# A two-layer trunk on one core: the mask by ScalarE, joint head products, rows' inverse roots by ScalarE, and turns between two blocks of the output projection

## The chip, the cores and the metric

The kernel runs on one core of one Trainium2 chip. The metric is the time of one execution on the device in microseconds (us). Engines are named as in the profile: PE is TensorE's matmul, PEld its weight loads, DVE VectorE, ACT ScalarE, SP the queue that issues nearly all DMAs.

## The reference

Two layers (DEPTH = 2) work on x, 256 rows by 2048 columns, all in float32. Cut to what matters here:

```
shift, scale, gate = split(c @ w_ada + b_ada)
h = rms_norm(x, g_pre) * (1 + scale) + shift
u, g_pool, q, k, v, g_diff = split(h @ w_in)             # 2048 -> 6144 columns
pool = multiscale_pool(u, w_pool, pool_scale) * silu(g_pool)     # 4 groups
q, k = rope(q), rope(k)                                  # 8 heads, 2 maps of 64 columns each
s = q k^T / 8, set to -1e30 where chunk(key) > chunk(query), chunks of 64 rows
p = softmax(s);  a = p[map 0] - lam * p[map 1]
diff = rms_norm(a v, subln_g) * (1 - lam_init) * silu(g_diff)
y = concat(pool, diff) @ w_out                           # 2048 -> 2048 columns
x = x + (1 + gate) * rms_norm(y, g_post)
rms_norm(x, g) = x * rsqrt(mean(x * x) + 1e-6) * g
```

## The kernel before

Rows are held as two tiles of 128 (st = 0, 1). The big products, h @ w_in and y = cat @ w_out, run in a split float32: each weight tile (`raw`, 128x1024) is cast to a rounded high part on ACT (`whi`), the rest is taken on DVE (`wlo`), and PE adds three products, high by high, high by low and low by high, of 128x512 each. A *unit* is two such 128-row slices of a 512-column block `nb`: 12 products of 512 columns for both row tiles. `plan()` writes the order of all units by hand: 12 blocks of w_in in each layer, then w_out. Lines 489 to 499 lay out w_out: the first half of the sum (k of the four pool groups, cat 0 to 3) for blocks 0, 1, 2, 3, then the second half (the four pairs of heads, cat 4 to 7) for blocks 2, 3, 0, 1. In the last eight units of a layer (a group of their own) row tile 0 runs through all before row tile 1.

All other work is written as tasks (`Flow`, lines 132 to 333). A planner at build time holds a clock for each engine, estimates when each task's next instruction can start from what it reads and writes (`depends`, line 273), and picks the one to be issued next by a due time. The order so found is the fixed order in which each engine takes its instructions on the chip; an instruction that isn't ready there holds up those behind it on its engine. The unit stream (`products`) has the latest due of all, so that on PE whatever else is ready goes first. `depends` makes the first product into a PSUM bank wait until that bank is free, bank by bank.

Each head of the attention (`head`, line 1202) takes two of four PSUM banks (`self.banks`), one for each map m. Query tile t = 0 sees 128 keys, t = 1 sees 256. Lines 1211 to 1213 make four float32 products with 64 rows of the array each, in the order (m, t) = (0,0), (1,0), (0,1), (1,1); each shows as two MATMUL rows, `psb<-zz,zz`. Lines 1214 to 1216 then add the mask by one bf16 product for each map, `psb<-neg,ind`. DVE takes the negated row maximum of each part (`top`), ACT the exponential with its sum (`exp`). `heads` (line 1233) runs two heads as a pair, at most two pairs at a time. It subtracts the maps, transposes them, multiplies by v, takes the rows' inverse roots (`rsqrt` with n = 4, on DVE), gates, transposes again and writes cat 4 to 7.

`rms` (line 796) makes the inverse root of each row's mean square for the norms before and after a layer: a `tensor_reduce` and then `rsqrt` with n = 1, in all eight short instructions on DVE (a start value from the bits, three Newton steps of two instructions). It is called six times: for x at the start (two row tiles), for y and for the next x between the layers (two each), and for y at the end (two). `residual` (line 1389) calls it after y; the last one is followed by x = y * r + x and by the stores.

Of the kernel before, what the change touches and what calls it, by code (L numbers as in the profile page):

```python
# [13 lines left out]
BF16 = mybir.dt.bfloat16  # L14
# [6 lines left out]
DEPTH = 2  # L21
S = 256
D = 2048
P = 128
# [58 lines left out]
class Task:  # L83
# [3 lines left out]
    def __init__(self, flow, f, due):  # L87
        self.flow, self.f, self.due = flow, f, due
        self.ask, self.cond, self.error, self.over = None, None, None, False
# [40 lines left out]
class Flow:  # L130
# [8 lines left out]
    TABLES = ((AF.Exp, 1), (AF.Silu, 2), (AF.Sin, 3))  # L139
# [29 lines left out]
    def due(self, due):  # L169
        self.cur.due = due if callable(due) else lambda: due  # L170

# [75 lines left out]
    def turn(self, key, op, outs, ins, total, table):  # L247
# [7 lines left out]
        a.names = {r[0] for r in a.outs + a.ins}  # L255
# [19 lines left out]
    def depends(self, a):  # L275
        t = 0.0
        for r in a.ins:
            t = max(t, self.latest(self.wrote, r))
            if a.key != "tensor" and r[0].startswith(("acc", "ps")):
                t = max(t, self.latest(self.used, r))  # L280
        for r in a.outs:
            if a.key != "tensor" or not self.wrote.get(r[0]):
                t = max(t, self.latest(self.used, r))
        return t
# [113 lines left out]
class Kern:  # L398
# [39 lines left out]
    def plan(self):  # L438
# [25 lines left out]
        for l in range(DEPTH):  # L464
# [35 lines left out]
            while l + 1 < DEPTH and kp_at[l + 1][self.START[l + 1] - 1] is None:  # L500
                take()
        for l, n in enumerate(self.TURN):
# [62 lines left out]
    def run(self):  # L565
# [9 lines left out]
        self.pairs, self.turning, self.mixed = 0, 0, [0] * DEPTH  # L575
# [6 lines left out]
    def begin(self):  # L582
# [17 lines left out]
        self.sqj = self.const([P, NB], "sqj", BF16)  # L600
        self.arrived, self.squared = [False] * NST, False
# [68 lines left out]
    def mask(self):  # L670

        v = self.nc.vector
# [100 lines left out]
    def rsqrt(self, ss, n, mul=None, end=None):  # L773


        v = self.nc.vector
        x, h = ss, self.small([P, n], "rh")
# [3 lines left out]
        if mul:  # L781
            x = self.small([P, n], "rx")
            v.tensor_scalar(x, ss, 0.5 * mul, 0.5 * EPS, op0=ALU.mult, op1=ALU.add)
        v.tensor_scalar(yi, x.bitcast(I32), -0.5, 0x5F3759DF - (1 << 22) - (1 << 31), op0=ALU.mult, op1=ALU.add)
        for i in range(3):
            if n == 1:
                v.scalar_tensor_tensor(h, y, x, y, op0=ALU.mult, op1=ALU.mult)
            else:
                v.tensor_tensor(h, y, y, op=ALU.mult)
                v.tensor_tensor(h, h, x, op=ALU.mult)  # L790
            if i == 2 and end is not None:
                v.tensor_tensor(y, y, end, op=ALU.mult)
# [409 lines left out]
    def head(self, l, h0, qT, kT, st, p):  # L1202

        nc, v = self.nc, self.nc.vector
# [24 lines left out]
    def heads(self, l, hp):  # L1229
# [232 lines left out]
```

## Time and profile before

| | us |
|---|---|
| runs of the kernel before | 826.73, 826.27, 825.59; median 826.27 |
| the profiled execution, its own time | 826.03 |
| its span, from first to last instruction | 824.2 |
| PE, DVE, ACT busy in it | 803.8, 703.2, 535.7 |

A row of a timeline gives the start in us from the span's start, the time taken, the engine, the instruction with what it writes and reads, how many of them were merged, and in brackets the idle time before it with what ended that. All lines of the kernel are recorded at line 125, a helper's, so tiles tell instructions apart: `accc` holds sums of the big products, `psb` the banks of the small ones, `zz` the blocks of h @ w_in, `catz` the input of w_out, `sm`, `rs`, `rh`, `ry` short columns. Matmuls are pipelined, so that what a matmul costs is read from start to start and not from its own duration.

### The profile page before, as it was taken

To read this page: it belongs to the slowest core of one execution; us is meant where nothing else is said; L and a number is where in the kernel's file an instruction comes from. 1 tells how busy PE (TensorE), PEld (TensorE's weight loads), DVE (VectorE), ACT (ScalarE), POOL (GpSimd) and SP (SyncE) were. 2 spreads that over 40 slices of the span, in tenths; PEclk is the share of its full clock that TensorE was granted. 3 is DMA by queue.
4 is the path that set the end of the run, shared out by engine and by line. 5 is a ranking of instruction groups with operands and counts; after the bars stand their busy time and mean duration, and the time that the engine had idled before them with its cause. 6 is when DMAs were issued, how large, how long until landed. Compare 5 with 4: busy or idle time off the path is not lost.

```text
span 824.2 us, 11857 instructions
## 1 busy us (share of the span) xinstructions
PE 803.8 (98%) x4064; PEld 662.2 (80%) x4064; DVE 703.2 (85%) x1262; ACT 535.7 (65%) x930; POOL 0.2 (0%) x4
## 2 busy tenths in 40 slices
PE   7999999999999999999999999999999999999995
PEld 3688788888998777788878889888898887778884
DVE  7999999899989889899899899879888997678814
ACT  3779998777665566766388557657565466677511
POOL 0000000000000000000000000000000000000000
PEclk9999999999999999999999999999999999999998
DMA  9999997999998776877898599999999974545303
GB/s 346 407 410 409 408 373 278 395 392 371 390 375 298 258 236 223 275 257 254 299 337 316 201 391 366 335 368 366 335 393 381 349 257 118 183 139 179 125 1 102
DMA packets 68383, 245.07 MB, mean 297 GB/s; under 512 B 7746, under 2 KB 8034, under 8 KB 68066
## 3 DMA queue, kind: packets, MB, share of 16 engines
q1 hardware_dynamic: 68034, 244.14, 81.5%
q8 instruction: 32, 0.52, 0.2%
q10 hardware_dynamic: 288, 0.17, 0.1%
q14 instruction: 29, 0.23, 0.1%
HBM read 242.17 MB, written 2.11 MB: 296 GB/s over the span
## 4 chain that ended last, share of the span: by engine, by line
PE 94%; DVE 3%; ACT 1%; DMA 1%; issue 0%; SPq 0%; DVEq 0%; ACTq 0%
PE accc L125 85%; PE psb L125 9%; DVE adaz L125 1%; DMA adaz<-in_w_ada 1%; DVE wloz L125 0%; ACT halfz L125 0%; ACT zz L125 0%; DVE x L125 0%; DVE rh L125 0%; DVE ry L125 0%; PE accb L125 0%; ACT accc L125 0%; DVE zz L125 0%; DVE halfz L125 0%; ACT hz L125 0%
## 5 line engine op out<-in xcount | busy, mean ns | idle before, releaser
L125 PE MATMUL accc<-whiz,hz 128*128 128x512 f32 x1256 | 397.8, 394 | 2.5 <-ACT accc L125 1.2
L125 DVE TENSOR_TENSOR wloz<-rawz,whiz 128x1024 fp32r<-128x1024 f32 x253 | 304.1, 1220 | 16.1 <-ACT whiz L125 13.1
L125 ACT CAST whiz<-rawz 128x1024 fp32r<-128x1024 f32 x253 | 260.5, 1055 | 85.7 <-DMA rawz<-in_w_in 55.6
L125 PEld LDWEIGHTS accc<-whiz,hz 128*128 128x128 f32 x1256 | 234.4, 188 | 56.3 <-DVE hz L125 3.4
L125 DVE SCALAR_TENSOR_TENSOR adaz<-adaz,cb 128x1024 f32<-128x1024 f32 x192 | 231.0, 1220 | 25.7 <-DMA adaz<-in_w_ada 23.5
L125 PE MATMUL accc<-wloz,hz 128*128 128x512 f32 x628 | 246.6, 393 | 0.0
L125 PE MATMUL accc<-whiz,catz 128*128 128x512 f32 x512 | 165.6, 398 | 0.9 <-DVE catz L125 0.9
L125 PEld LDWEIGHTS accc<-wloz,hz 128*128 128x128 f32 x628 | 118.0, 188 | 24.7 <-DVE wloz L125 1.0
L125 PEld LDWEIGHTS accc<-whiz,catz 128*128 128x128 f32 x512 | 94.9, 188 | 21.4 <-DVE catz L125 1.3
L125 PE MATMUL accc<-wloz,catz 128*128 128x512 f32 x256 | 101.7, 397 | 0.0
L125 ACT COPY zz<-accc 128x512 f32<-128x512 f32 x121 | 70.1, 588 | 35.7 <-PE accc L125 35.3
L125 ACT COPY accc<-zz 128x512 f32<-128x512 f32 x106 | 62.7, 592 | 24.8 <-DVE halfz L125 19.4
L125 PE MATMUL accc<-hz,whiz 128*128 128x256 f32 x512 | 72.2, 283 | 0.0
L125 PEld LDWEIGHTS accc<-hz,whiz 128*128 128x128 f32 x512 | 66.7, 192 | 0.7
L125 PEld LDWEIGHTS accc<-wloz,catz 128*128 128x128 f32 x256 | 48.2, 188 | 10.0 <-issue 0.5
L125 PE MATMUL accc<-hz,wloz 128*128 128x256 f32 x256 | 41.4, 283 | 0.0
L125 ACT ACTIVATE sqj<-accc 128x512 bf16<-128x512 f32 x16 | 9.6, 600 | 41.8 <-PE accc L125 41.6
L125 PEld LDWEIGHTS accc<-hz,wloz 128*128 128x128 f32 x256 | 35.4, 192 | 0.0
L125 DVE TENSOR_TENSOR yz<-accc,Gz 128x512 f32<-128x512 f32 x16 | 10.8, 688 | 28.6 <-ACT sqj L125 28.5
L125 ACT ACTIVATE halfz<-psb,sm 128x128 f32<-128x128 f32 (+1 forms) x64 | 26.5, 421 | 10.9 <-DVE sm L125 7.2
L125 PE MATMUL psb<-consts,halfz 128*128 128x128 f32 x176 | 30.4, 276 | 3.0 <-ACT halfz L125 3.0
L125 PEld LDWEIGHTS psb<-consts,halfz 128*128 128x128 f32 x176 | 22.2, 141 | 11.5 <-ACT halfz L125 5.4
(109 smaller groups left out, 530.0 us busy)
## 6 DMA issues: line engine op xcount, KB each, us to landing
adaz<-in_w_ada SPq DMA_DIRECT2D x192, 512.0 KB, 6.8
rawz<-in_w_in SPq DMA_DIRECT2D x189, 512.0 KB, 6.5
rawz<-in_w_out SPq DMA_DIRECT2D x64, 512.0 KB, 4.2
x<-in_x SPq DMA_DIRECT2D x2, 1024.0 KB, 8.5
wpz<-in_w_pool SPq DMA_DIRECT2D x4, 512.0 KB, 7.2
Gz<-gate SPq DMA_DIRECT2D x4, 512.0 KB, 4.8
out<-x SPq DMA_DIRECT2D x8, 256.0 KB, 2.8
rawz<-in_w_in SPq DMA_DIRECT2D x6, 256.0 KB, 8.9
```

What stands on the lines that cost most here:

```text
L125: return f(*args, **kw)
```

## The change

1. **Mask.** `mask` makes one float32 tile `neg` of 64x2x64. In `head` the two mask products are gone; after a map's last product ACT copies `neg` over the masked quarter of both parts of its bank, and `top` reads the bank after that.
2. **Joint head products.** A new `until` tells the planner to hold the next instruction of a task until given tiles are written and given banks are free. `head` names q, k and both its banks ahead of its first product. It adds no instruction and no wait on the chip.
3. **Inverse roots.** `rms` is now: a negated `tensor_reduce` on DVE, a square root on ACT, a reciprocal and one Newton step of two instructions on DVE. ACT's table for the root is loaded by a dummy root (`root_table`): at the start, and in each layer after the eighth head's exponentials, due 6 us ahead of the layer's last eight units of w_out, once the gate blocks have been through Silu. The planner's list of tables has a new entry for it. `rsqrt` for the heads keeps its instructions.
4. **Turns.** The first eight units of w_out in each layer are sorted by k // 4: blocks 0 and 1 with cat 0 and 1, then blocks 0 and 1 with cat 2 and 3.

```diff
+    TABLES = ((AF.Exp, 1), (AF.Silu, 2), (AF.Sin, 3), (AF.Sqrt, 4))
...
+    def until(self, *tiles, free=()):
+        self.cur.also = [(self.wrote, self.region(x)) for x in tiles] + [(self.used, self.region(x)) for x in free]
...
     def depends(self, a):
...
+        for d, r in a.also:
+            t = max(t, self.latest(d, r))
         return t
...
     def plan(self):
...
+            i = next(i for i, u in enumerate(units) if (u.w, u.l) == ("w_out", l))
+            units[i : i + 8] = sorted(units[i : i + 8], key=lambda u: u.k // 4)
...
     def begin(self):
...
+        self.one, self.junk1 = self.const([P, 1], "one"), self.const([P, 1], "junk1")
+        nc.vector.memset(self.one, 1.0)
+        self.root_table()
...
     def mask(self):
-        self.ind = self.const([P, P], "ind", BF16)
-        v.memset(self.ind, 0.0)
-        self.neg = self.const([P, 2, CHUNK], "neg", BF16)
-        v.memset(self.neg, NEG)
-        for m in range(2):
-            v.memset(self.ind[m * DQK : m * DQK + 1, 0:CHUNK], 1.0)
+        self.neg = self.const([CHUNK, 2, CHUNK], "neg")
+        self.nc.vector.memset(self.neg, NEG)
...
-    def rms(self, parts):
-        s1 = self.small([P, 1], "rs1")
-        self.nc.vector.tensor_reduce(s1, parts, axis=AX.X, op=ALU.add)
-        return self.rsqrt(s1, 1)
+    def rms(self, parts, due=None):
+        v, f = self.nc.vector, self.f
+        s1, y, h = (self.small([P, 1], n) for n in ("rs", "ry", "rh"))
+        v.tensor_reduce(s1, parts, axis=AX.X, op=ALU.add, negate=True)
...
+        self.nc.scalar.activation(y, s1, AF.Sqrt, scale=-2.0)
+        v.reciprocal(y, y)
...
+        v.scalar_tensor_tensor(h, y, s1, y, op0=ALU.mult, op1=ALU.mult)
+        v.scalar_tensor_tensor(y, h, 1.5, y, op0=ALU.add, op1=ALU.mult)
+        return y
+
+    def root_table(self):
+        self.nc.scalar.activation(self.junk1, self.one, AF.Sqrt)
...
     def head(self, l, h0, qT, kT, st, p):
...
+        f.until(qT, kT, free=bank)
         for t, o in ((0, slice(0, P)), (1, slice(P, 3 * P))):
             for m, r in maps:
-                nc.tensor.matmul(bank[m][:, o], qT[r, t, c], kT[r, 0 : t + 1, c], start=t == 0, stop=False, skip_group_check=True)
-        for m, r in maps:
-            o = bank[m].rearrange("p (t k) -> p t k", t=2)[:, :, CHUNK:P]
-            nc.tensor.matmul(o, self.ind[r, :], self.neg[r, :, :], start=False, stop=True, skip_group_check=True)
+                nc.tensor.matmul(bank[m][:, o], qT[r, t, c], kT[r, 0 : t + 1, c], start=t == 0, stop=t == 1, skip_group_check=True)
+        for m in range(2):
+            nc.scalar.copy(bank[m].rearrange("p (t k) -> p t k", t=2)[0:CHUNK, :, CHUNK:P], self.neg)
...
     def heads(self, l, hp):
...
+                self.weighed[l] += 1
+                if self.weighed[l] == H:
+                    f.due(self.need(next(u for u in self.units if u.group == 2 * l + 2), 6.0))
+                    f.wait(lambda: all((l, b) in self.done for b in GP + GD))
+                    self.root_table()
```

## Rows read from the trace of the kernel before

**Rows 1.** The page's busy times, and of its slices over the span the clock granted to TensorE (tenths of full speed).

```profile
PE 803.8 (98%) x4064; PEld 662.2 (80%) x4064; DVE 703.2 (85%) x1262; ACT 535.7 (65%) x930; POOL 0.2 (0%) x4
...
PEclk9999999999999999999999999999999999999998
```

**Rows 2.** The page's chain of work that ended last, as shares of the span by engine.

```profile
PE 94%; DVE 3%; ACT 1%; DMA 1%; issue 0%; SPq 0%; DVEq 0%; ACTq 0%
```

**Rows 3.** Busy time by stretch of 40 us, in both of which heads run. The columns: the stretch, its length, then busy us and in brackets the number of instructions of PE, PEld, DVE, ACT and POOL, the clock granted to TensorE, the share of DMA and GB/s.

```profile
340.00:380.00 40.00, 40.00 (x216) 31.84 (x215) 34.75 (x109) 27.18 (x71) 0.00 (x0) 1.00 0.86 286
...
720.00:760.00 40.00, 40.00 (x230) 31.84 (x229) 31.14 (x90) 30.00 (x89) 0.00 (x0) 1.00 0.51 154
```

**Rows 4.** Timeline of PE in the plain stream of w_out, late in layer 1.

```profile
801.02 0.39 PE L125 MATMUL accc<-wloz,catz 128*128 128x512 f32 x1
...
801.70 0.39 PE L125 MATMUL accc<-wloz,catz 128*128 128x512 f32 x1
```

**Rows 5.** Timeline of PE where a head's first product stands by itself: the first such place of the trace, then one head of layer 0 with both its places, then the last of the 13 such places.

```profile
274.12 0.48 PE L125 MATMUL psb<-zz,zz 64*128 64x128 f32 x2
...
321.70 0.40 PE L125 MATMUL accc<-wloz,catz 128*128 128x512 f32 x1
322.02 0.48 PE L125 MATMUL psb<-zz,zz 64*128 64x128 f32 x2
322.44 0.73 PE L125 MATMUL accc<-whiz,catz 128*128 128x512 f32 x2
...
323.70 0.40 PE L125 MATMUL accc<-wloz,catz 128*128 128x512 f32 x1
324.03 0.70 PE L125 MATMUL psb<-zz,zz 64*128 64x128 f32 x5
...
324.93 0.73 PE L125 MATMUL accc<-whiz,catz 128*128 128x512 f32 x2
...
745.31 0.49 PE L125 MATMUL psb<-zz,zz 64*128 64x128 f32 x2
```

**Rows 6.** Timeline of PE around a head of layer 1 whose products stand together.

```profile
694.60 0.40 PE L125 MATMUL accc<-wloz,hz 128*128 128x512 f32 x1
694.93 0.93 PE L125 MATMUL psb<-zz,zz 64*128 64x128 f32 x8
695.69 0.22 PE L125 MATMUL psb<-neg,ind 64*128 64x128 bf16 x2
695.84 0.73 PE L125 MATMUL accc<-whiz,hz 128*128 128x512 f32 x2
```

**Rows 7.** Timeline of DVE at a head's first maximum in layer 1.

```profile
748.73 0.62 DVE L125 TENSOR_REDUCE sm<-psb 128x1 f32<-128x128 f32 x2 [1.14 <-PE psb L125]
```

**Rows 8.** Groups of instructions with shapes kept apart: busy us, mean ns of one, idle us before them. ACT's table loads, and the short instructions nearest to the new ones.

```profile
L125 ACT ACT_TABLE_LOAD x6 | 7.7, 1283 | 5.4 <-DVE sm L125 2.7 <-DMA cb<-in_c 2.6
...
L125 ACT COPY grow<-psb 16x128 f32<-16x128 f32 x2 | 0.5, 248 | 0.2 <-PE psb L125 0.2
...
L125 ACT ACTIVATE lamexp<-lamdots 128x4 f32<-128x4 f32 x1 | 0.2, 193 | 0.0
```

**Rows 9.** Timeline of PE and DVE where layer 0 of w_out waits for cat.

```profile
319.26 0.68 DVE L125 TENSOR_TENSOR catz<-zz,catz 128x512 fp32r<-128x512 f32 x1
...
319.99 0.73 PE L125 MATMUL accc<-whiz,catz 128*128 128x512 f32 x2 [0.88 <-DVE catz L125]
```

**Rows 10.** Timeline of DVE and PE between the layers: three weight tiles' rest on DVE, and PE's wait for the low part of h.

```profile
418.47 3.48 DVE L125 TENSOR_TENSOR wloz<-rawz,whiz 128x1024 fp32r<-128x1024 f32 x3
...
422.21 0.73 PE L125 MATMUL accc<-whiz,hz 128*128 128x512 f32 x2 [0.93 <-DVE hz L125]
```

**Rows 11.** Timeline of DVE at the end: the first two of the inverse root's eight instructions, which stand in a row, and the final x behind them.

```profile
815.98 0.15 DVE L125 TENSOR_REDUCE rs<-yss 128x1 f32<-128x5 f32 x1
816.16 0.15 DVE L125 TENSOR_SCALAR ry<-rs 128x1 int32<-128x1 int32 x1
...
817.70 2.74 DVE L125 SCALAR_TENSOR_TENSOR x<-yz,ry,x 128x512 f32<-128x512 f32 x4
```

**Rows 12.** The start: issues of w_ada's tiles in the first 30 us (count, KB each, median us from issue to landing), the issues of the fifth to the eighth tile (merged), DVE on the eighth, and PE's wait behind it.

```profile
adaz<-in_w_ada SPq DMA_DIRECT2D x12, 512.0 KB, 9.5
9.28 4.15 SPq L125 DMA_DIRECT2D adaz<-in_w_ada  x4
22.92 1.22 DVE L125 SCALAR_TENSOR_TENSOR adaz<-adaz,cb 128x1024 f32<-128x1024 f32 x1
25.28 3.70 PE L125 MATMUL accc<-rawz,halfz 128*128 128x512 f32 x8 [1.23 <-ACT halfz L125]
```

**Rows 13.** Timeline of ACT at a table load: the load and the instruction behind it.

```profile
31.74 1.28 ACT L125 ACT_TABLE_LOAD   x1
33.03 0.35 ACT L125 ACTIVATE cos<-halfz,halfpi 128x64 f32<-128x64 f32 x1
```

**Rows 14.** Timeline of DVE in layer 1: the last pair of heads' inverse roots, first and last instruction (those between are left out), and the last part of cat; of PE the last product of the kernel.

```profile
762.55 0.16 DVE L125 TENSOR_SCALAR rx<-sm 128x4 f32<-128x4 f32 x1
...
770.42 0.16 DVE L125 SCALAR_TENSOR_TENSOR ry<-rh,ry 128x4 f32<-128x4 f32 x1
...
775.85 0.75 DVE L125 SCALAR_TENSOR_TENSOR catz<-psb,cols,catz 128x512 fp32r<-128x512 f32 x1 [0.69 <-ACT catz L125]
...
814.17 0.39 PE L125 MATMUL accc<-whiz,catz 128*128 128x512 f32 x1
```

More of the change, by code (lines that the diff above doesn't have):

```diff
@@ L88, in __init__ @@
         self.flow, self.f, self.due = flow, f, due
-        self.ask, self.cond, self.error, self.over = None, None, None, False
+        self.ask, self.cond, self.error, self.over, self.also = None, None, None, False, []
         self.go = threading.Semaphore(0)
@@ L138 @@
     COST = {"vector": (0.09, 1.08e-3, 0.02, 0.15), "scalar": (0.11, 0.92e-3, 0.13, 0.18), "gpsimd": (0.25, 2.3e-3, 0.0, 0.15)}
-    TABLES = ((AF.Exp, 1), (AF.Silu, 2), (AF.Sin, 3))
+    TABLES = ((AF.Exp, 1), (AF.Silu, 2), (AF.Sin, 3), (AF.Sqrt, 4))
     TABLE_US = 1.29
@@ L254, in turn @@
         a.outs, a.ins = [self.region(x) for x in outs], [self.region(x) for x in ins]
-        a.names = {r[0] for r in a.outs + a.ins}
+        a.also, self.cur.also = self.cur.also, []
+        a.names = {r[0] for r in a.outs + a.ins} | {r[0] for _, r in a.also}
         a.dep, a.f32 = None, key == "tensor" and op == "matmul" and ins[-1].dtype == F32
@@ L574, in run @@
         self.gated = [[0] * NST for _ in range(DEPTH)]
-        self.pairs, self.turning, self.mixed = 0, 0, [0] * DEPTH
+        self.pairs, self.turning, self.mixed, self.weighed = 0, 0, [0] * DEPTH, [0] * DEPTH
         self.wps, self.G, self.nlam, self.band = [None] * DEPTH, [None] * DEPTH, None, None
@@ L670, in mask @@
     def mask(self):
-        v = self.nc.vector
-        self.ind = self.const([P, P], "ind", BF16)
-        v.memset(self.ind, 0.0)
-        self.neg = self.const([P, 2, CHUNK], "neg", BF16)
-        v.memset(self.neg, NEG)
-        for m in range(2):
-            v.memset(self.ind[m * DQK : m * DQK + 1, 0:CHUNK], 1.0)
+        self.neg = self.const([CHUNK, 2, CHUNK], "neg")
+        self.nc.vector.memset(self.neg, NEG)
     def late_constants(self):
@@ L771, in copy, with rsqrt @@
             self.nc.scalar.copy(out, x)
-    def rsqrt(self, ss, n, mul=None, end=None):
+    def rsqrt(self, ss, n, mul, end):
         v = self.nc.vector
-        x, h = ss, self.small([P, n], "rh")
+        x, h = self.small([P, n], "rx"), self.small([P, n], "rh")
         yi = self.small([P, n], "ry", I32)
         y = yi.bitcast(F32)
-        if mul:
-            x = self.small([P, n], "rx")
-            v.tensor_scalar(x, ss, 0.5 * mul, 0.5 * EPS, op0=ALU.mult, op1=ALU.add)
+        v.tensor_scalar(x, ss, 0.5 * mul, 0.5 * EPS, op0=ALU.mult, op1=ALU.add)
         v.tensor_scalar(yi, x.bitcast(I32), -0.5, 0x5F3759DF - (1 << 22) - (1 << 31), op0=ALU.mult, op1=ALU.add)
         for i in range(3):
[L786 to L791, printed above, removed]
+            v.tensor_tensor(h, y, y, op=ALU.mult)
+            v.tensor_tensor(h, h, x, op=ALU.mult)
+            if i == 2:
                 v.tensor_tensor(y, y, end, op=ALU.mult)
@@ L794, in rsqrt @@
         return y
-    def rms(self, parts):
-        s1 = self.small([P, 1], "rs1")
-        self.nc.vector.tensor_reduce(s1, parts, axis=AX.X, op=ALU.add)
-        return self.rsqrt(s1, 1)
+    def rms(self, parts, due=None):
+        v, f = self.nc.vector, self.f
+        s1, y, h = (self.small([P, 1], n) for n in ("rs", "ry", "rh"))
+        v.tensor_reduce(s1, parts, axis=AX.X, op=ALU.add, negate=True)
+        if due is not None:
+            f.due(due)
+        self.nc.scalar.activation(y, s1, AF.Sqrt, scale=-2.0)
+        v.reciprocal(y, y)
+        if due is not None:
+            f.due(-7.0)
+        v.scalar_tensor_tensor(h, y, s1, y, op0=ALU.mult, op1=ALU.mult)
[3 more added lines that the diff above has]
+        self.nc.scalar.activation(self.junk1, self.one, AF.Sqrt)
     ROOT = 2.0**-6
@@ L1202, in head @@
     def head(self, l, h0, qT, kT, st, p):
-        nc, v = self.nc, self.nc.vector
+        nc, v, f = self.nc, self.nc.vector, self.f
         c = slice(h0 * P, (h0 + 1) * P)
```

## The prediction, made before the change was built

> **What bounds the kernel now.** I read the page first: PE is busy 98% of the span at full clock throughout, DVE 85%, ACT 65% [rows 1], and the chain that ended last is 94% PE [rows 2]. A busy PE is not yet a PE at its peak, so I next read the plain stream by starts: two starts that are three products apart lie 0.68 us apart [rows 4], 0.227 us for each product of 512 columns. Wherever the stream runs undisturbed it keeps that pace. So the time is, roughly, PE's start, the sum of what PE issues, its few waits, and the tail behind its last product. An instruction taken from PE is worth its start-to-start time; one taken from another engine is worth nothing, except where PE or the tail waits for it. I therefore looked for three things: what the small products of the heads cost PE, where PE waits, and what follows its last product.
>
> **Joint head products.** At the head in the middle of rows 5, PE makes the product (m, t) = (0,0) by itself, goes back to the stream, and makes the other three with the mask two microseconds later. Start to start, less the 0.23 of the stream's own product, the first piece costs 322.44 - 321.70 - 0.23 = 0.51 us, the second 324.93 - 323.70 - 0.23 = 1.00: 1.51 together [rows 5]. Where all four stand together with the mask, it is 695.84 - 694.60 - 0.23 = 1.01 [rows 6]. The reasons show in the rows: eight 64-row matmuls take 0.76 us side by side (694.93 to 695.69), two alone 0.42, since the two maps use different halves of the array and run together; and each step from the stream to a 64-row product costs 0.10 more than the stream's pace (322.02 - 321.70 = 0.33 here, by starts, against 0.23). Of the 16 heads 13 stand in two places, from the pair at 274.12 to that at 745.31 [rows 5], 3 in one. The planner asks for each bank separately: bank 0 is free earlier, so the first product goes early. Nothing uses it early: the first maximum reads a bank that is complete with its mask, and waits for PE just after it [rows 7]. `until` holds the first product until bank 1 is free too, which is when the second piece went anyhow. So 13 x (1.51 - 1.01) = **6.5 us** come off PE. Bounds: 0 if something else still slips between, 6.5 if none does; I take 6.5 because the planner puts the four in a row once all are ready, the stream being always last. Behind the held product only its own task waits; no instruction on any queue is held on the chip, since the wait is the planner's.
>
> **Mask off PE.** In a joint head the mask lasts from 695.69 to 695.84, 0.15 us [rows 6]. The way back from 64-row products to the stream costs something whoever is last: a lone 64-row matmul before the stream takes 0.2 (two take 0.42 [rows 5]) against 0.76 / 8 = 0.1 side by side. So between 0.05 and 0.15 is saved in each of 16 heads; 0.06 is nearest, as the mask's own columns are a quarter of those of the last product: **1.0 us** (0.8 to 2.4). In exchange ACT makes 32 copies of 64x128 into PSUM. The nearest row, a copy of 16x128, takes 0.248 us [rows 8]: 8 us, 4 in each layer. ACT is busy 27 to 30 of 40 us where heads run [rows 3], so it fits. Each copy waits for PE in ACT's queue; behind it stand the casts of weight tiles, and PE waits for those a few us later. `top` now waits for ACT too: about 0.3 us more in each head's chain. I cost both at nothing because 10 of 40 us of ACT cover the first, and the slack of the next paragraph the second; without cover, see the rivals.
>
> **What comes due next.** If PE's stream arrives some 3.7 us earlier in each layer's heads, the heads must be as much earlier. In layer 1 the last cat is complete at 776.6; its first use is the fourth unit of the second half, so 13 units of 12 products lie behind it: 814.4 - 13 x 2.72 = 779.0 [rows 4, 14]. The slack is only 2.4 us. But the chain is stretchable: that pair's inverse roots, a dozen instructions of 0.16 us, lie spread from 762.55 to 770.58 [rows 14], with weight tiles of 1.2 us placed between them since nothing was urgent; an earlier due time closes them up, and DVE has 5 to 9 idle us in 40 [rows 3].
>
> **Turns.** In layer 0 PE waits 0.88 us for cat 2 [rows 9]. With turns, two units of block 1 (5.4 us) come ahead of that use, more than the wait. **0.9 us** (0 to 1.0); in layer 1 nothing waits there. The accumulators of block 1 are wanted 5.4 us earlier, and those of block 0 come free 5.4 us later; an eviction reads a bank of 128x512, as the final 2.74 us for four such reads on DVE, 0.7 each [rows 11], so I cost this at nothing.
>
> **Inverse roots.** The eight instructions take 817.70 - 815.98 = 1.72 us in a row [rows 11]. The new chain: reduce 0.18 by starts, hand-off 0.05 (as from DVE to PE, 319.94 to 319.99 [rows 9]), root about 0.19 as the nearest activation of a few columns [rows 8], hand-off 0.05, reciprocal and two Newton instructions at the mean of the eight, 1.72 / 8 = 0.215 each: 1.12. At the tail ACT is idle, so **0.6 us** (0.3 to 0.75) is gained in full. Between the layers four such roots are in line, two for each row tile, and PE waits 0.93 us for h there; but what it waits behind is a stretch of 3.48 us of weight tiles on DVE [rows 10], a placing that may fall better or worse: **0.4 us** (-1.0 to 0.9). A root can also stand behind a weight cast on ACT. At the start PE waits 1.23 us behind the eighth tile of w_ada: its issue ended by 13.4, 9.5 us later is 22.9, and DVE took it at 22.92 [rows 12]. That wait is DMA's, so shorter DVE work ahead of it gives little: **0.2 us** (0 to 0.3).
>
> **Tables.** Two more loads come (root after Exp in each layer; the one at the start takes the place of the first load). A load takes 1.28 us [rows 8], and the next instruction starts with it, 31.74 + 1.28 = 33.02 against 33.03 [rows 13]. They are due 6 us ahead of the last eight units, when the heads are over, and I cost them at nothing, 0 to 2.6 us. The Trainium skill, in "ScalarE: Activation LUTs", What ACT_TABLE_LOAD costs, asks for some 1.38 us of drain beside each load, 2.66 in all, and its section on table sets speaks against going back and forth between Exp and the root; with that the upper end would be 5.3 us in place of 2.6, but the row shows no such drain.
>
> **Sum.** 6.5 + 1.0 + 0.9 + 0.6 + 0.4 + 0.2 = 9.6 us. A new order also opens new waits; of those that PE's timeline shows now, the size is 0.9 [rows 9, 10], and I set half a microsecond against the sum: 9.1. The profiled execution took 826.03 us (1.8 more than its span), 0.24 under the median of the runs; 826.27 - 9.1 = 817.2, and I say **817.0**.
>
> **Rivals.**
> - *The heads give it back.* The heads' chain doesn't close up, and the last cat stays at its time; PE then waits, and each layer gains only the slack, some 2.4 us, in place of 3.7. With 0.9 of turns no longer of use, 4.8 + 0.6 + 0.4 + 0.2 = 6: 820.3, or 822 if the copies delay the heads by another 0.8 a layer. For it: two engines now hand each bank on, and pairs wait for banks. Against: the spread-out roots. 0.15.
> - *The joint products don't come*, because other ready work goes between them. Then some 1 us of mask, and 2 of the rest remain: 823. 0.07.
> - *Slower: ACT becomes what PE waits for.* A mask copy that waits for PE holds a weight cast behind it, and PE runs out of weights. If every head made PE wait for one weight instruction (1.16 us, 3.48 / 3 [rows 10]), that is 16 x 1.16 = 18.6 us lost against 9.1 gained: 836. It turns slower from 9.1 / 16 = 0.57 us a head. For it: ACT takes its instructions in order, and it already waits for PE often. Against: 10 us idle in 40. 0.06, and another 0.02 for a worse order elsewhere.
> - *The tables cost*: 1.28 twice, on the path: 819.6. With the page's 2.66 it would be 822.3; 0.04 for both.
> - *More than forecast*: PE's small waits around the heads go with the splits: 812 to 813. 0.08.
>
> **How the numbers follow.** The forecast (813.5 to 820) has 0.58. What this kernel's measurement can tell from no change is about 0.2%, 1.65 us. Faster by over that: forecast 0.58, heads 0.15, tables 0.04, more 0.08, and most of the unjoined case 0.05: 0.90. Within it: 0.03; slower 0.07. For 8 in 10 the range takes the forecast, the heads' case and the tables: 813.0 to 822.0; its low end is the sum with the upper bounds of mask and roots.
>
> **What would show it.** Right: no `psb<-neg,ind`; in PE's timeline eight `psb<-zz,zz` matmuls in a row for all 16 heads, about 0.95 us from stream to stream; 32 new ACT copies of 0.25 us; no wait for catz at the start of w_out; 1.1 us from the last reduce to the final x. Wrong: lone pairs of `psb<-zz,zz`; PE waiting for catz at cat 6 and 7, for whi or for wlo in the heads' stretches; a table load ahead of a late root. The prediction as a whole fails if PE's waits grow by what its work shrinks.

## The result and the profile after

Measured side by side, the kernel before took 826.5 us (median of 6 runs) and the changed one 819.62 (6 runs, 819.3 to 822.77): a ratio of 0.9923, interval [0.9907, 0.994]. Run again later it took 820.64 against 826.84, 0.9926 [0.9913, 0.994]. The forecast was 817.0 in a range of 813 to 822. So sign and range held; the gain came out at 6.9 and 6.2 us in place of 9.3.

The profiled execution of the changed kernel is the longest of its six (822.77), so rows of form are taken from it, but time is accounted with the profiled execution of the repeat (820.13, span 818.4).

Busy times, clock slices and the chain of the changed kernel's page, to be held against [rows 1, 2]:

```profile
PE 796.9 (97%) x4032; PEld 657.0 (80%) x4032; DVE 693.3 (84%) x1223; ACT 549.7 (67%) x980; POOL 0.2 (0%) x4
...
PEclk9999999999999999999999999999999999999998
...
PE 84%; DMA 9%; DVE 3%; ACT 2%; issue 1%; SPq 0%; DVEq 0%; ACTq 0%
```

PE lost 6.9 busy us and its 32 mask products; ACT has 14 us more. The chain of this execution goes 9% through transfers instead of 1%, of w_ada and w_in by its list: where PE waits longer, it is followed to these. In the repeat, 2.6 us shorter, it is 3%. The heads look as forecast. All 16 stand in one place, eight 64-row matmuls in a row (timeline of PE, for [rows 5, 6]):

```profile
327.60 0.39 PE L125 MATMUL accc<-whiz,catz 128*128 128x512 f32 x1
327.92 0.93 PE L125 MATMUL psb<-zz,zz 64*128 64x128 f32 x8
328.77 0.51 PE L125 MATMUL accc<-whiz,catz 128*128 128x512 f32 x1
```

From stream to stream that is 328.77 - 327.60 - 0.23 = 0.94, against 1.51 for a split head and 1.01 for a joint one before. Over all 16 heads, added up from every place where a 64-row product stands (29 places before, 16 in the repeat), the heads' products cost PE 23.3 us before and 15.4 in the repeat, 7.9 less, if the 0.23 is taken off only where a product of the stream stands ahead (six places before and two in the repeat have a smaller one there), and 22.0 and 15.0, 7.0 less, if it is taken off everywhere. Joint products and mask were forecast at 7.5.

The copies and table loads that ACT got in exchange (groups with shapes kept apart: busy us, mean ns; idle before), for [rows 8]:

```profile
L125 ACT ACT_TABLE_LOAD x8 | 10.3, 1283 | 4.1 <-DVE sm L125 2.4 <-PEq L1473 1.6
...
L125 ACT COPY psb<-neg 64x128 f32<-64x128 f32 x32 | 7.5, 261 | 9.9 <-PE psb L125 9.9
```

A copy takes 261 ns (forecast 250); ACT stood 9.9 us in front of them, waiting for PE. The end, for [rows 11]: from the reduce to the final x it is 814.42 - 813.36 = 1.06 us, forecast 1.12, before 1.72.

```profile
813.36 0.15 DVE L125 TENSOR_REDUCE rs<-yss 128x1 f32<-128x5 f32 x1
813.54 0.20 ACT L125 ACTIVATE ry<-rs 128x1 f32<-128x1 f32 x1 [0.82 <-DVE rs L125]
813.78 0.16 DVE L125 RECIPROCAL ry<-ry 128x1 f32<-128x1 f32 x1 [0.27 <-ACT ry L125]
...
814.42 2.74 DVE L125 SCALAR_TENSOR_TENSOR x<-yz,ry,x 128x512 f32<-128x512 f32 x4
```

Where did the rest go? I took the n-th product into the big sums in both traces (3444 in each) and followed how its start moved, the repeat against before. That splits the 5.9 us by which the spans differ:

| stretch | forecast | measured |
|---|---|---|
| start, to the first product of the w_in stream | -0.2 | +1.3 |
| heads of layer 0 | | -6.0 |
| heads of layer 1 | | -2.9 |
| both layers' heads (joint, mask, turns) | -8.4 | -8.9 |
| between the layers | -0.4 | +1.4 |
| body of layer 1 ahead of its heads | 0 | +0.9 |
| tail | -0.6 | -0.6 |
| allowance for new waits | +0.5 | (in the lines above) |
| sum | -9.1 | -5.9 |

The parts that take work from PE or from the tail came as forecast. What failed stands in the lines in which only waits, and the clock behind them, can move: start, layer boundary, body of layer 1. Together they were forecast at -0.1 with the allowance, and gave +3.6. These lines in rows. At the start of the repeat (timeline of PE, then the stretch 25 to 30 us: busy us and counts of the five engines, granted clock, DMA share, GB/s), for [rows 12]:

```profile
19.85 1.98 PE L125 MATMUL accc<-rawz,halfz 128*128 128x512 f32 x4 [0.55 <-ACT halfz L125]
...
24.91 5.40 PE L125 MATMUL accc<-rawz,halfz 128*128 128x512 f32 x8 [2.22 <-ACT halfz L125]
...
31.46 0.79 PE L125 MATMUL accc<-whiz,hz 128*128 128x512 f32 x1
```

```profile
25.00:30.00 5.00, 5.00 (x8) 2.13 (x9) 4.13 (x7) 5.00 (x10) 0.00 (x0) 0.66 1.03 412
```

Row tile 1 is ready 1.4 us sooner (19.85; before, its products began at 21.21), and so PE then waits longer for w_ada's eighth tile: 2.22 us in place of 1.23. That alone would cost nothing; its eight products even start a little sooner than before (25.28). But behind the longer wait they take 5.40 us in place of 3.70. The 0.66 of the row is a mean: over 26 to 29 us the granted clock is 0.50, the level of 1.2 GHz, and it is 1.00, that of 2.4 GHz, over 25.0 to 25.6 and over 29.1 to 30. Before, it was 1.00 throughout. The stream begins at 31.46 instead of 30.13.

Between the layers (timelines of DVE and of PE in the repeat), for [rows 10]:

```profile
426.62 2.35 DVE L125 TENSOR_TENSOR wloz<-rawz,whiz 128x1024 fp32r<-128x1024 f32 x2
...
428.89 1.22 DVE L125 SCALAR_TENSOR_TENSOR adaz<-adaz,cb 128x1024 f32<-128x1024 f32 x1
...
430.03 1.12 DVE L125 TENSOR_TENSOR hz<-halfz,hz 128x128 fp32r<-128x128 f32 x4
```

```profile
428.43 0.50 PE L125 MATMUL accc<-whiz,hz 128*128 128x512 f32 x1 [0.29 <-ACT hz L125]
...
430.37 0.73 PE L125 MATMUL accc<-whiz,hz 128*128 128x512 f32 x2 [1.21 <-DVE hz L125]
```

The roots are shorter, and the wait of 0.93 us before the first products with h is gone: by the n-th product 1.1 us are gained there. But a dozen us further on the low part of h again stands behind weight work on DVE, 430.03 - 426.62 = 3.41 us of it, and PE waits 0.29 us and then 1.21 us. By starts these two places lose 2.5 us, so that 1.4 are lost in all. In the body of layer 1 the 0.9 us go at one new wait for ACT (PE of the repeat):

```profile
527.12 0.33 PE L125 MATMUL psb<-consts,halfz 128*128 128x128 f32 x1 [0.62 <-ACT halfz L125]
```

Within the heads of layer 0, at the first half of w_out, the wait of [rows 9] is gone, as turns promised: PE runs from 311.21, its first product with cat there, to beyond 320 with no gap. But two like it have come at the second half (PE of the changed kernel, idle 0.45 each; the repeat lists the same two, 0.9 us in all):

```profile
374.17 0.50 PE L125 MATMUL accc<-whiz,catz 128*128 128x512 f32 x1 [0.45 <-DVE catz L125]
...
378.12 0.50 PE L125 MATMUL accc<-whiz,catz 128*128 128x512 f32 x1 [0.45 <-DVE catz L125]
```

### The profile page after: what moved, and what is told of

Its sections match the earlier page's. It is cut to its first block, busy times and chain, and to the rows that moved or that the text cites. A ratio compares the mean times of both kernels' runs of the same rounds, so it can differ in the third digit from the quotient of the medians.

```text
span 821.0 us, 11817 instructions
## 1 busy us (share of the span) xinstructions
PE 796.9 (97%) x4032; PEld 657.0 (80%) x4032; DVE 693.3 (84%) x1223; ACT 549.7 (67%) x980; POOL 0.2 (0%) x4
## 4 chain that ended last, share of the span: by engine, by line
PE 84%; DMA 9%; DVE 3%; ACT 2%; issue 1%; SPq 0%; DVEq 0%; ACTq 0%
PE accc L125 76%; PE psb L125 8%; DMA adaz<-in_w_ada 5%; DMA rawz<-in_w_in 4%; DVE wloz L125 1%; DVE adaz L125 1%; ACT whiz L125 1%; DVE zz L125 0%; ACT zz L125 0%; ACT halfz L125 0%; DVE rh L125 0%; SPq L125 0%; DVE x L125 0%; DVE ry L125 0%; ACT accc L125 0%
## 5 line engine op out<-in xcount | busy, mean ns | idle before, releaser
L125 ACT COPY zz<-accc 128x512 f32<-128x512 f32 x128 | 74.2, 585 | 25.2 <-PE accc L125 24.4
L125 ACT COPY accc<-zz 128x512 f32<-128x512 f32 x109 | 64.4, 592 | 24.6 <-DVE halfz L125 17.8
L125 ACT ACTIVATE halfz<-psb,sm 128x128 f32<-128x128 f32 x64 | 26.3, 421 | 2.4 <-DVE sm L125 0.9
```

The costliest lines, as they stand in the source:

```text
L125: return f(*args, **kw)
```

## The experiments

The planner fixes each engine's order and also which of ACT and DVE takes each eviction of a bank; I call both together the order. My theory after the result: joint products are nearly the whole gain; what is missing was lost not to the new instructions but to the order that the planner finds once anything in its input changes. Rivals: the gain is a sum of four parts, each worth something; or ACT's added work (copies, roots, loads) costs what is missing.

### Each part alone, replanned

**e1**: the kernel before with `until` and its call in `head`; **e2**: with the mask by ACT; **e3**: with the new `rms` and `root_table`; **e4**: with the sort of w_out's first eight units. Each is that part of the diff ahead of the prediction and nothing else. The runs come in three groups, e1 to e4, e5 to e8 and e9 to e12, each on one chip with its own runs of the kernel before beside it.

> The kernel before with the joint head products alone. The forecast's own working: 13 split heads lose 0.5 us each, so 6.5 us less than before, and no lone pair of 64-row matmuls is left in PE's timeline. The rival that the heads give it back: PE's work shrinks by those 6.5 us, but PE waits for cat in the second half of w_out and only some 4 us of it reach the time. The rival that the order is what counts: all 16 heads stand together and PE's work shrinks by 6.5, but the new order opens waits elsewhere, so that the time moves by anything from 3 to 8 us.

> The kernel before with the mask by ScalarE alone. The forecast's working: 32 mask products go from PE, 32 copies of about 0.25 us come to ScalarE, 1.0 us less (0.8 to 2.4). The rival that ScalarE becomes what PE waits for: PE's waits for weight tiles or for cat grow where heads run, and the time is 1 us or more above before. The order rival: within 2 us of before on either side, with the heads still in two places.

> The kernel before with the rows' inverse roots by ScalarE's root alone, its two table loads with them. The forecast's working: 0.6 us less at the tail, 0.4 between the layers, 0.2 at the start, 1.2 in all. The rival formed on the changed kernel's trace: the second row tile's root at the start is 0.7 us shorter, PE gets to its wait for w_ada that much sooner and waits longer, the granted clock behind that wait falls to half and the next products take 0.85 us in place of 0.43, so that the start costs 1.5 to 2 us and the whole is 0 to 1 us slower than before. In the profile: granted clock of 25 to 30 us at 1.00 (forecast) or near 0.66 (rival), and PE's 80th product of the big sums at 39.6 us (forecast) or 41 to 42 us (rival).

> The kernel before with the turns of the first two blocks of w_out alone. The forecast's working: PE's wait of 0.88 us for cat 2 in layer 0 goes, 0.9 us less; nothing in layer 1. The order rival: that wait goes, but others of its size come, so that the time is within 1.5 us of before on either side.

| | median, us | ratio to before (826.4) |
|---|---|---|
| e1, joint by the planner | 827.85 | 1.0025 [1.0012, 1.0038] |
| e2, mask by ACT | 829.34 | 1.0042 [1.0029, 1.0055] |
| e3, roots | 838.59 | 1.015 [1.0135, 1.0166] |
| e4, turns | 830.59 | 1.0049 [1.0036, 1.0062] |

Every part by itself makes the kernel slower: 1.5 + 2.9 + 12.2 + 4.2 = 20.8 us for the four, which together gain 6 to 7. Replanned parts don't add up to the change. My forecasts had all four faster; a loss stood only in rivals, of 1 us or more for e2, of at most 1 us for e3 and 1.5 for e4. Rows show what happens in e1, where PE's instructions are the same but for their order (PE and the stretch 320 to 325, then ACT and PE at 650; the profiled execution, 831.44, is the longest of its 12):

```profile
321.64 0.79 PE L125 MATMUL accc<-whiz,catz 128*128 128x512 f32 x1 [1.90 <-ACT catz L125]
```

```profile
320.00:325.00 5.00, 3.36 (x14) 2.10 (x15) 5.00 (x17) 3.07 (x12) 0.00 (x0) 0.62 0.51 183
```

```profile
647.16 1.05 ACT L125 CAST whiz<-rawz 128x1024 fp32r<-128x1024 f32 x1 [1.58 <-DVE wloz L125]
649.50 1.04 ACT L125 CAST whiz<-rawz 128x1024 fp32r<-128x1024 f32 x1 [1.29 <-DVE wloz L125]
650.45 0.58 ACT L125 COPY zz<-accc 128x512 f32<-128x512 f32 x1
```

```profile
651.08 0.76 PE L125 MATMUL psb<-band,zz 128*128 128x144 f32 x4 [3.23 <-ACT zz L125]
```

The second case shows how an order costs time. The copy that PE waits for needs nothing new, but it stands on ACT behind two weight casts, and each of these waits for DVE to give a buffer back. PE waits 3.23 us for a copy of 0.58. In the first case a wait of 1.90 us is followed by a granted clock of 0.62. Against e5 below, which has the same products on PE, the waits in PE's list come to 17.3 us in place of 11.2, and the granted clock, 0.62 and 0.69 over 320 to 330 us and 0.73 and 0.93 over 650 to 660, costs up to 5.2 more; the two profiled executions differ by 13.0. In e2, by the n-th product, 1.3 us go in the heads of both layers, 1.2 between the layers and 0.5 in the body of layer 1: so the rival in which PE waits for ACT where heads run isn't the whole of it. e3 has such waits ahead of and among layer 0's heads (1.54 and 1.19 us on PE),

```profile
313.29 1.20 PE L125 MATMUL psb<-band,zz 128*128 128x144 f32 x8 [1.54 <-ACT halfz L125]
...
323.85 0.50 PE L125 MATMUL accc<-whiz,catz 128*128 128x512 f32 x1 [1.19 <-ACT catz L125]
```

and by the n-th product is 7.3 us behind there; 2 us of that come back, 1 goes between the layers, and 6.6 more in the heads of layer 1. The rival formed for e3 failed at the start: PE waits 1.44 us for w_ada, the granted clock stays at 1.00 over 25 to 30 us, and the 80th product stands at 39.3 us, where the forecast said 39.6 and the rival 41 to 42. So the new roots alone don't bring the fall of the clock there. e4 puts a weight cast whose transfer is late on ACT ahead of the rows' scaling that PE needs next; PE waits 2.10 us for it, until 505.30, and the granted clock is 0.66 over 505 to 510 us:

```profile
503.79 1.04 ACT L125 CAST whiz<-rawz 128x1024 fp32r<-128x1024 f32 x1 [3.06 <-DMA rawz<-in_w_in]
504.74 0.50 ACT L125 ACTIVATE halfz<-x,ry 128x256 f32<-128x256 f32 x1
```

### The same parts with the order kept

**e5** asks the planner for the same instructions as before and gets the order of before on every engine; only the issue of a head's first product is held back until its second:

```diff
+        held = []
         for t, o in ((0, slice(0, P)), (1, slice(P, 3 * P))):
             for m, r in maps:
-                nc.tensor.matmul(bank[m][:, o], qT[r, t, c], kT[r, 0 : t + 1, c], start=t == 0, ...)
+                x = bank[m][:, o], qT[r, t, c], kT[r, 0 : t + 1, c]
+                self.f.turn("tensor", "matmul", [x[0]], list(x[1:]), False, [])
+                held.append((x, t == 0))
+                if len(held) > 1 or m or t:
+                    for y, first in held:
+                        nc.tensor.eng.matmul(*y, start=first, stop=False, skip_group_check=True)
+                    held = []
```

**e6** plans the mask products as before but issues ACT's copy in their place; **e8** is both:

```diff
-            nc.tensor.matmul(o, self.ind[r, :], self.neg[r, :, :], start=False, stop=True, ...)
+            self.f.turn("tensor", "matmul", [o], [self.neg, self.ind[r, :]], False, [])
+            nc.scalar.eng.copy(bank[m].rearrange("p (t k) -> p t k", t=2)[0:CHUNK, :, CHUNK:P], self.neg)
```

**e7** leaves the work of before as it is and changes only one estimate of the planner. That gives another order, in which three of ACT's 930 instructions, net, have gone to DVE:

```diff
-    COST = {..., "scalar": (0.11, 0.92e-3, 0.13, 0.18), ...}
+    COST = {..., "scalar": (0.12, 0.92e-3, 0.13, 0.18), ...}
```

> The kernel before, its planner untouched and every engine's order kept, except that each head's first product is issued right ahead of its second, so that the four stand together. This is the joint products without a new order. Theory (PE's work counts, the order adds waits of its own): PE gets its 6 to 6.5 us back and nothing new is opened, 4.5 to 6.5 us less than before. Rival (the heads give it back): PE's work shrinks by 6 us but PE waits for cat, and the time is within 2 us of before.

> The kernel before, its planner untouched and every engine's order kept, except that where the planner put a mask product on PE, a copy by ScalarE of 64x128 is issued in its place. This is the mask by ScalarE without a new order. Theory (the 3.5 us lost with the mask alone came from the new order): 0 to 2 us less than before. Rival (ScalarE's copies hold up weight casts): 1 us or more above before, with PE's waits for weight tiles grown where heads run.

> The kernel before with the planner's estimate of one ScalarE instruction's fixed time at 0.12 us in place of 0.11; no instruction is added, taken away or changed, only the order that the planner finds. Theory (each new order brings waits of its own): the time moves by 2 us or more, most likely up, since the order of before has few waits. Rival (the edits themselves cost what was measured): within 1 us of before.

> The kernel before with its order kept, and both the joint issue of the four products and ScalarE's copies in place of the mask products. Theory: the two add up to the forecast's 7.5 us of PE, and 5 to 7.5 us come off the time, about 820. Rival (given back by the heads or by ScalarE): less than 3 us.

| | median, us | ratio to before (826.93) |
|---|---|---|
| e5, joint, order kept | 818.79 | 0.9907 [0.9892, 0.9922] |
| e6, mask, order kept | 826.58 | 0.9997 [0.9984, 1.0009] |
| e7, nothing but another order | 830.68 | 1.0044 [1.0028, 1.0061] |
| e8, joint and mask, order kept | 818.69 | 0.9912 [0.9893, 0.9931] |

The same edit takes 818.79 us in the old order (e5) and 827.85 in a new one (e1). In e5 a head looks like a joint one of before (timeline of PE), and PE's waits (us in total, times, longest) are those of before, which lists the same six groups with 3.0, 2.7, 1.8, 1.2, 1.1 and 0.9:

```profile
322.04 0.93 PE L1218 MATMUL psb<-zz,zz 64*128 64x128 f32 x8
322.80 0.22 PE L125 MATMUL psb<-neg,ind 64*128 64x128 bf16 x2
```

```profile
PE psb L125 <- ACT halfz L125: 3.5, 2, 3.0
PE psb L125 <- DMA cb<-in_c: 2.7, 1, 2.7
PE accc L125 <- ACT halfz L125: 1.8, 2, 1.2
PE accc L125 <- ACT accc L125: 1.2, 3, 0.7
PE accc L125 <- DVE hz L125: 1.1, 2, 0.9
PE accc L125 <- DVE catz L125: 0.9, 1, 0.9
```

By the n-th product, e5 stays level with before until the heads, is 3.9 us ahead behind those of layer 0, keeps that through layer 1 up to its heads, and gains 3.7 more in these: 7.6 in all, of which 6.3 to 6.8 lie at the places of the 64-row products (22.0 to 15.6 with 0.23 off everywhere, 23.3 to 16.5 otherwise). The rest stands just behind them. The second product of the stream after a break starts 0.33 us after the first, not 0.23: before, the stream is back at 322.44 [rows 5], and its third product stands here (PE), 0.56 us on, where 0.45 would be the plain pace:

```profile
323.00 0.39 PE L125 MATMUL accc<-wloz,catz 128*128 128x512 f32 x1
```

By the n-th product the start of the stream moves by 0.51 us at such a place and by 0.10 to 0.12 more one product later. So a break that goes is worth 0.61, and 13 of them 7.9. With 8.1 by the medians e5 gave more than the 4.5 to 6.5 expected, and e8 with 8.2 more than its 5 to 7.5.

The mask gives 0.35 us by the medians of e6, nothing that its interval can tell from none, and e8 no more than e5 (0.9912 against 0.9907). By the n-th product e6's profile gains 0.75 us in the heads, but it began 0.6 late, ahead of any head; e8's gains 0.6 over e5 in the heads, and loses 0.5 ahead of those of layer 1 and 0.2 at the start. e7 shows the price of an order: 3.8 us for no change of work at all. By the n-th product 3.3 us of it go in the heads of layer 1; an early loss is a weight tile that comes late to PE:

```profile
82.74 0.50 PE L125 MATMUL accc<-wloz,hz 128*128 128x512 f32 x1 [0.84 <-DVE wloz L125]
```

### The roots, the start, and the changed kernel's own order

**e9** is e5 with the new roots in the planned places of the old eight instructions (the trace has eight such roots, two in each of the four places that the text on the kernel before lists, where it counts six calls); the dummy root of the table follows the eighth head's exponentials:

```diff
+        plan = lambda op, out, *ins: f.turn("vector", op, [out], list(ins), False, [])
+        plan("tensor_reduce", s1, parts)
+        v.tensor_reduce(s1, parts, axis=AX.X, op=ALU.add, negate=True)
+        plan("tensor_scalar", y, s1)
+        a.activation(y, s1, AF.Sqrt, scale=-2.0)
+        plan("scalar_tensor_tensor", h, y, s1, y)
+        v.reciprocal(y, y)
...
```

**e10** is the changed kernel again. **e11** is the changed kernel with eight transposes, whose output nobody reads, put on PE ahead of the products that wait for w_ada; every other instruction keeps its place:

```diff
+                if sts == [1] and ks == [0] and u is self.units[self.count - 1]:
+                    for n in range(8):
+                        nc.tensor.eng.transpose(self.fill, self.ident, self.ident)
```

**e12** is the changed kernel with the one estimate of e7 changed; five of ACT's 980 instructions, net, go to DVE.

> The kernel before with its order kept and the joint issue of the head products, and with the rows' inverse roots by ScalarE's root in the places that the planner gave the old eight instructions (dummy roots load the table right behind the eighth head of each layer). The forecast's size of the roots: 0.6 us at the tail, up to 0.9 between the layers and 0.2 at the start, so 0.6 to 1.5 us below the joint products alone (818.8): 817.3 to 818.2. Rival (the roots cost time by themselves, as their run alone showed 12 us more): 2 us or more above the joint products alone.

> The changed kernel once more. Theory: what lay between its profiled execution (822.8) and its other runs (819.5) is the fall of the clock behind the wait for w_ada at the start, 1.7 us, and two waits for late transfers in layer 1 (2.6 us by starts at 502 and 528 us); a profile of an execution near 819.5 has neither or only one of these. Rival: the clock falls there in every execution, since the shorter root of the second row tile makes PE's wait longer; then granted clock is near 0.66 in 25 to 30 us again.

> The changed kernel, its order kept, with eight transposes of the identity on PE ahead of the products that wait for w_ada at the start (some 1.6 us of work nobody reads). If the clock falls there in every execution of the changed kernel: 1.5 us less than the changed kernel run beside it, granted clock 1.00 in 25 to 30 us. If it falls seldom: the same time as the changed kernel within 0.7 us.

> The changed kernel with the planner's estimate of one ScalarE instruction's fixed time at 0.12 us in place of 0.11; the instructions are the same, the order another. Theory (the order counts for several us whatever the edits): it moves by 2 us or more, to either side, most likely up to 822 to 827. Rival (the changed kernel's order is nothing special): within 1 us of the changed kernel run beside it.

| | median, us | ratio to before (826.84) |
|---|---|---|
| e9, joint and roots, order kept | 818.47 | 0.9894 [0.988, 0.9908] |
| e10, changed kernel again | 820.64 | 0.9926 [0.9913, 0.994] |
| e11, changed, PE kept busy at the start | 819.78 | 0.9913 [0.9896, 0.9929] |
| e12, changed, another order | 825.47 | 0.998 [0.9967, 0.9992] |

**e9.** Against e5 its profile gains what was forecast for the roots: 0.4 us at the start (where e6 and e8, with the old roots, lie 0.6 and 0.2 behind e5), 0.95 between the layers, where e5's wait of 0.94 us for h is gone, and 0.66 at the tail. But in layer 1 it falls back by 0.6 us at 551 and by 1.9 between 638 and 655, with new waits for two results of ACT (timelines of PE, and of ACT ahead of the first):

```profile
640.89 0.76 PE L125 MATMUL psb<-band,zz 128*128 128x144 f32 x4 [0.81 <-ACT zz L125]
...
646.34 1.99 PE L125 MATMUL psb<-halfz,wpz 128*128 128x256 f32 x8 [0.54 <-ACT halfz L125]
```

```profile
632.90 1.05 ACT L125 CAST whiz<-rawz 128x1024 fp32r<-128x1024 f32 x1 [3.52 <-DMA rawz<-in_w_in]
```

So even with the order kept the 2 us are given back in that execution. By the medians 0.3 us remain (1.1 by the ratios), within the intervals, where 0.6 to 1.5 were expected. But for the roots and the loads ACT's instructions stand in the same order as in e5, and what makes them late is a transfer: the weight cast at 632.90 waits for its tile of w_in, while in e5 it starts at 631.09. The DMA is busy throughout there (share 1.00 over 610 to 650 us in e9, 0.99 to 1.01 in e5). So the two results aren't late by the roots' or the loads' own time on ACT; why the transfer comes later isn't shown.

**e10.** Its profiled execution is 2.6 us shorter than that of the changed kernel, and the clock fell at the start in both, as the rival said. By the n-th product 1.9 of the 2.6 us lie at the two places in layer 1 that the theory named: at 502 us the wait is gone, at 527 it is 0.62 us in place of 1.55.

**e11** keeps the clock (PE, and the stretch 25 to 30 us):

```profile
23.20 1.04 PE L1117 MATMUL psb<-consts 128*128 128x128 f32 x8
25.36 3.70 PE L125 MATMUL accc<-rawz,halfz 128*128 128x512 f32 x8 [1.12 <-ACT halfz L125]
...
30.22 0.79 PE L125 MATMUL accc<-whiz,hz 128*128 128x512 f32 x1
```

```profile
25.00:30.00 5.00, 4.64 (x11) 2.20 (x12) 3.80 (x8) 5.00 (x10) 0.00 (x0) 1.00 1.02 408
```

With eight small matmuls in the wait, 1.12 us of it are left idle, the clock stays at 1.00, the same eight products take 3.70 us, and the stream begins at 30.22, 1.24 sooner than in e10. That is the start's loss, in one execution. Across the kernel it is worth less: the profile is 1.3 us ahead as far as 410 us and back level at 656, behind waits that are longer or new (1.05 us at 526.40, where e10 waits 0.62, and 0.53 at 642.01, which e10 doesn't have). The medians differ by 0.9 us, between the two cases of the expectation, with overlapping intervals, so a gain in time is not shown.

**e12** loses 4.8 us against e10, most of what the change had gained, with the same work but for those five. In the profiles (3.3 us apart) its start is 1.3 us better, and the clock there stays at 1.00 behind a wait of 1.70 us. By the n-th product that has shrunk to 0.2 ahead of the heads of layer 0; these lose 2.2 us, and those of layer 1 lose 1.9. Between the layers it loses nothing against e10: it waits there for a weight tile, as below, where e10 waits for h:

```profile
428.58 0.50 PE L125 MATMUL accc<-wloz,hz 128*128 128x512 f32 x1 [1.55 <-DVE wloz L125]
```

## Why the prediction was right, and which of its terms was mis-sized

- **Joint products, 6.5: right, and too small.** 29 places with 64-row products became 16. By themselves (e5) they are worth 8.1 us, by the medians more than the whole change, though the intervals overlap. The sum priced a break by 0.51 us and left out 0.10 at the second product behind it, so that its upper bound of 6.5 was too low. That nothing slips between, and that nobody uses the first product early, held for all heads.
- **Mask, 1.0: right in PE's rows, not seen in the time.** A joint head costs 0.94 to 0.95 in place of 1.01, 0.06 a head as reckoned, so 1 us of PE in 16 heads, of which the profiles of e6 and e8 show 0.75 and 0.6 in the heads; but by the medians the two show 0.35 and 0.1 us of time, less than their intervals tell. The rival in which ACT becomes the bound didn't come: with the order kept, 32 copies, 9.9 us of which ACT spends waiting in the changed kernel, cost nothing measurable.
- **What comes due next: the outcome was right, the reason wasn't.** No wait for a late cat of layer 1 stands in PE's list; in layer 0 two of 0.45 us came. But the chain did not close up, and didn't have to. From the start of the last 64-row product to the end of the last cat it took 776.60 - 748.31 = 28.3 us before, 769.00 - 740.71 = 28.3 in e5 and 770.01 - 741.79 = 28.2 in the repeat. The whole chain came earlier with the products of PE that feed it. In e5 even the last pair's inverse roots are spread as before (DVE; those between are left out), for [rows 14]:

```profile
754.96 0.16 DVE L125 TENSOR_SCALAR rx<-sm 128x4 f32<-128x4 f32 x1
...
762.83 0.16 DVE L125 SCALAR_TENSOR_TENSOR ry<-rh,ry 128x4 f32<-128x4 f32 x1
...
768.25 0.75 DVE L125 SCALAR_TENSOR_TENSOR catz<-psb,cols,catz 128x512 fp32r<-128x512 f32 x1 [0.69 <-ACT catz L125]
```

So the slack of 2.4 us was no limit: in the rival that has the heads give it back, the last cat stays at its time, and it doesn't.
- **Turns, 0.9: the wait went, the gain didn't follow.** The two new waits for cat take 0.9 back, and turns alone cost 4.2 us (e4); that the order around them did it fits the rows of e4 but wasn't tested apart. What the sort would be worth in a kept order wasn't tried, since it is itself an order.
- **Roots.** Tail 0.6: right (1.06 us from reduce to x; e9 shows 0.66 too). Between the layers I named the risk, a placing that may fall worse by as much as 1.0, and took +0.4; it fell worse by 1.4, beyond that bound. At the start I had costed a wait ended by a transfer at nothing beyond its end. What I left out is that the clock can fall behind a wait: +1.3. The roots alone don't do that: in e3 and e9 PE waits 1.44 and 1.23 us there and the clock stays at 1.00. In the repeat PE was already 1.0 us sooner at row tile 0 (its first product at 16.15, before 17.14); why isn't shown.
- **Tables: right.** Two more loads, no cost seen. A load's successor starts 1.30 us after it, here as in [rows 13]. The Trainium skill, in "ScalarE: Activation LUTs", What ACT_TABLE_LOAD costs, asks for 2.66 us a switch, drain included; the trace doesn't agree (timeline of ACT in the changed kernel):

```profile
364.13 1.28 ACT L125 ACT_TABLE_LOAD   x1
365.43 0.20 ACT L125 ACTIVATE junk<-one 128x1 f32<-128x1 f32 x1
```

- **The allowance for a new order, 0.5: the term that was mis-sized.** I took its size from the waits that the kernel before happened to have. Two pairs with equal work and different orders differ by 3.8 us (e7) and 4.8 (e12), and each part replanned by itself lost 1.5 to 12 us. The loss that the change took, by the lines that only waits and the clock can move, is 3.6 against the 0.1 gain forecast there. It should have stood as a term of some 4 us, since the planner's input changed in four ways at once, and "a worse order elsewhere" as far more likely than the 0.02 it got: all five other replannings of the kernel before (e1 to e4, e7) came out slower than it. That the range held is in part luck: the joint products gave 1.1 to 1.6 us more than their term, and the range was open above for the heads' rival, whose mechanism didn't come.

Why just this order turns out fair and those of e1 to e4 poor isn't explained by any of the four edits; the runs show only that it is so, and not whether the planner's estimates had once been chosen for the order of before. The best kernels run are e9 (818.47), e8 (818.69) and e5 (818.79), alike within their intervals. All three have medians below the changed kernel's two; e5 needs one part of the four.

## What to carry to other kernels

Where a build-time planner fixes the order on in-order queues, test an edit twice: replanned, and issued in the old order; the first alone measures the planner's luck, here 4 to 9 us, as much as the edit. Count what an edit takes from the bounding engine by starts at each place, the first products behind it included; here that part came true within 1.6 us. Give every term that lives on waits a range from a run with the same work in another order. Of a wait that grows ask also what clock follows it, and of a chain with little slack whether it is fed by what you are making earlier.

## What the runs showed of the hardware

- The clock fell at single waits of PE in the midst of work. Its mean over 5 us was 0.66 of full speed over 25 to 30 us behind an idle stretch of 2.22 us (e10) and of 2.02 (the changed kernel's first profile), 0.62 over 320 to 325 at one of 1.90 (e1) and 0.66 over 505 to 510 at one of 2.10 (e4); within it the clock is at one of its two levels, 0.50 over 26 to 29 us in e10 and 1.00 next to that. Over the same 25 to 30 it stayed at 1.00 behind 1.12 (e11), 1.23 (before), 1.44 (e3) and 1.70 us (e12). In the case of 2.22 against 1.23 us, 1 us more of waiting cost 1.7 us in the next eight products (5.40 against 3.70).
- The length of the wait alone doesn't decide it. In e3 the clock stays at 1.00 over 650 to 660 with a wait of 2.69 us that ends at 653.66, and is 0.66 over 325 to 330 behind one of 1.19 that ends at 323.85.
- A return of PE from 64-row products to the stream costs twice: the lone pair 0.51 us from stream to stream, and 0.10 more before the second product behind it.
- With eight unread transposes of 1.04 us in that wait (e11) the clock stayed at 1.00; that they shorten the whole isn't shown.
- A table load on ACT occupies it for 1.28 us, and behind each of the eight loads of the changed kernel the next instruction starts 1.29 to 1.30 us after the load's start.
